# Feed-forward of a streaming encoder layer: running-sum copies and second-layer additions traced with priority, two weight quarters split in pieces of 512 columns

## The chip, the cores and the metric

One NeuronCore of a Trainium2 chip runs the whole program in one launch. The metric is the device time of one execution in microseconds, the median of the runs shown: 977.34 us before the change (three runs, 976.65 to 977.91).

## What is computed

The reference is one layer of a hybrid encoder on two request groups (512 prompt tokens and 64 sample tokens, 576 together, model width 1024): a mixing stage (gated delta rule and differential attention), a cross-attention to a memory, and a feed-forward stage, then a last norm. The change lies in the feed-forward stage:

```
hn = _rmsnorm(h, p['ln_ffn'])
h = h + jnp.square(jax.nn.relu(hn @ p['w_ff1'])) @ p['w_ff2']
```

`w_ff1` is 1024 x 4096 and `w_ff2` is 4096 x 1024, all in float32. The kernel keeps float32 accuracy by splitting each operand into a high part (a cast to a rounded format, `F32R`) and a low part (the operand minus that cast), and adding three products: high x high, high x low, low x high.

## The kernel before, in words

**First layer.** The 4096 hidden columns are taken in 16 pairs of 128-column blocks (`ff1_pair(p, sx)`, L1469). A pair is a 2 x 2 block product: two halves of the model width and two halves of the tokens (`N0`, `N1`, 288 tokens each, `NH`). It is computed with seven block products instead of eight, in a Strassen-like scheme, from sums and differences of the activations (`B1`, `B2`, `T12`, `T34`, prepared earlier by `combine`) and of the weights. One `product(i, b, start)` is 12 matmuls of 288 columns (4 steps over 128 rows of the half width, times three high/low combinations). The order that is traced is 1, 5, 6, 2, 7, 3, 4. Products 1, 6, 7 and 4 go one after another into the same PSUM bank `x` (tag `ba`), which goes on accumulating: after products 1, 6 and 7 the bank holds a running sum that is needed on its own, so `keep(b)` (L1492) copies it to SBUF on ScalarE (L1494) before the next product may add to the bank. Product 5 goes into bank `z` (tag `g1`), is copied by `keep` as well, and product 3 is added later; product 2 has bank `y` (tag `gs`). `put` (L1497) then forms one block of the hidden layer: an addition on VectorE (L1502), relu and square on ScalarE (L1503, L1504), from pair 10 on a multiplication by the squared norm factor (L1506), a cast (L1508) and the low part (L1509).

**Weights of the first layer.** `load_pair(p)` (L1384) starts two loads of 512 KB, `raw` a and b; together they are the four quarters of the block. `split_pair(p)` (L1394) makes the seven weight operands: sums and differences on VectorE (L1402, L1407, L1408, L1415, in place in the raw tiles), and for each operand a cast on ScalarE and a low part on VectorE (`halves_to`, L1355; in the profile the cast is L1356 and the low part L1357). Five of the operands are 512 columns of a partition wide and are split one by one; the quarters in a (operands 6 and 7, tile tag `wl`) and those in b (operands 2 and 4, tag `w4`, shown as `w` in the profile) are split in one instruction of 1024 columns each. The destination tiles are the buffers of the pair that is being multiplied, so a cast can start when the products that read the old contents are done. `ff1_pair(p)` traces `split_pair(p + 1)` and `load_pair(p + 2)` at its end. For pair 0 there is a separate `split_first`, which the change leaves alone.

**Second layer.** The main loop (L1648) has 8 groups of two pairs. In group g, after every `ff1_pair`, four blocks `project(weights2(...), ..., add_group(g - 1, m), kt=4)` (L1653) multiply the hidden block of the group before by 128 columns of `w_ff2`: a first half of 256 tokens, whose bank holds two column halves side by side (the second is the `more` that the evacuation gets), and a second half of 320 tokens. Each half takes a bank of tag `pr`, of which there are three in turn. `weights2` (L1461) loads 256 KB and `split` (L1453) casts it (L1457) and takes the low part (L1458). `add_group` (L1535) gives the evacuation: for group 0 the sum is copied (`A.copy` at L1542, or `add_to` at L191, which copies `more` on ScalarE at L192 and adds on VectorE at L193); for the others it is added on VectorE into the running sum `am` (L1544) and, for the first half, the second part is added as well (L1546). A bank is free when its last reader is done.

**What sets the order.** Each engine runs its own queue in order. The order inside a queue is fixed when the program is built: a scheduler goes through the traced instructions with an estimate of their times and, whenever an engine is free, gives it the ready instruction with the smallest priority number. That number counts up in the order of tracing. Inside `with tc.high_priority():` the count starts again from the beginning of the program, so such an instruction goes ahead of every ready one without it; among themselves they go by their place in their own block. Before the change the casts and low parts in `split_pair` (for p above 1) and in `split` (where `urgent`) are traced so; `keep`, `put` and the evacuations in `add_group` are not.

Of the kernel before, what the change touches and what calls it, by code (L numbers as in the profile page):

```python
# [11 lines left out]
ALU = mybir.AluOpType  # L12
# [25 lines left out]
def hybrid_layer_kernel(  # L38
# [10 lines left out]
    V, A, G = nc.vector, nc.scalar, nc.gpsimd  # L49
# [50 lines left out]
    def bank(tag="ba"):  # L100
        return ps.tile([P, 512], F32, tag=tag, name=nm(tag), bufs=BANKS[tag])
# [4 lines left out]
    def mm(out, lhsT, rhs, start=True, stop=True, pin=False, skip_group_check=False):  # L106
        i = nc.tensor.matmul(out, lhsT, rhs, start=start, stop=stop, skip_group_check=skip_group_check)  # L107
        if pin:
            tc.keep_in_program_order(i)
# [81 lines left out]
    def add_to(dst, b, more):  # L191
        A.copy(dst, more)  # L192
        V.tensor_tensor(dst, b, dst, ALU.add)  # L193
# [302 lines left out]
    for a0, n in HALVES:  # L496
        b = bank("pr")
# [7 lines left out]
    b = bank()  # L505
# [49 lines left out]
    for j in range(3):  # L555
        b = bank()
# [713 lines left out]
    for k2 in range(KT // 2):  # L1270
        b = bank()
# [6 lines left out]
    for h in range(H):  # L1278
# [15 lines left out]
        for t, (q0, _) in enumerate(QT):  # L1294
            t0, n = TT[t]
            kk, kl = (mkT, mkl) if t < 4 else (cmT, cml)
            b = bank(("gs", "g0", "g1")[t % 3])
# [25 lines left out]
        for i in range(2):  # L1323
            b, b2 = bank(("g0", "gs")[i]), bank(("g1", "ba")[i])
# [14 lines left out]
    NH = T // 2  # L1339
# [8 lines left out]
    def ft(tag, shape, bufs, dt=F32):  # L1348
        return fp.tile(shape, dt, tag=tag, name=nm(tag), bufs=bufs)
# [5 lines left out]
    def halves_to(hi, lo, src):  # L1355
        A.copy(hi, src)  # L1356
        V.tensor_tensor(lo, src, hi.bitcast(F32), ALU.subtract)  # L1357
# [21 lines left out]
    def wtile(tag, shape, dt=F32R):  # L1379
        return wp.tile(shape, dt, tag=tag, name=nm(tag), bufs=3 if tag == "raw" else 2)  # L1380
# [3 lines left out]
    def load_pair(p):  # L1384

        raws[p] = raw = [wtile("raw", raw_, F32) for i in range(2)]
        for i in range(2):
            src = w_ff1[0, 512 * i : 512 * i + 512, 2 * P * p : 2 * P * (p + 1)]
            nc.sync.dma_start(raw[i], src.rearrange("(k p) n -> p k n", p=P))

    def low_and_high(t):
        return [t[:, 0], t[:, 1]]

    def split_pair(p):  # L1394


        a, b = raws.pop(p)
        A11, A21, A12 = a[:, :, :P], a[:, :, P:], b[:, :, :P]
        s1 = ft("s1", block_, 2)
        parts[p] = ws = {}  # L1400
        with tc.high_priority() if p > 1 else ExitStack():
            V.tensor_tensor(s1, A21, b[:, :, P:], ALU.add)  # L1402
            ws[1] = low_and_high(wtile("wh", wide_))
            halves_to(*ws[1], A11)
            ws[5] = low_and_high(wtile("wh", wide_))
            halves_to(*ws[5], s1)
            V.tensor_tensor(A21, A11, A21, ALU.subtract)  # L1407
            V.tensor_tensor(A11, s1, A11, ALU.subtract)  # L1408
            t = [wtile("wl", raw_) for _ in range(2)]
            halves_to(*t, a)  # L1410
            ws[6], ws[7] = ([x[:, :, c : c + P] for x in t] for c in (0, P))
            t = [ft("w4", raw_, 3, F32R) for _ in range(2)]
            halves_to(*t, b)
            ws[2], ws[4] = ([x[:, :, c : c + P] for x in t] for c in (0, P))
            V.tensor_tensor(A12, A12, A11, ALU.subtract)  # L1415
            ws[3] = low_and_high(ft("w4", wide_, 3, F32R))
            halves_to(*ws[3], A12)
# [51 lines left out]
    def ff1_pair(p, sx):  # L1469
        ws = parts.pop(p)  # L1470

        def of(x, n):
            return lambda j, k: x[j][:, n, k, :]

        def half(u, n):
            return lambda j, k: u[:, j, k, n]

        operands = {
            1: lambda j, k: B1[k // 2][:, j, k % 2, :], 2: half(B2, N0), 3: half(B2, N1),
            4: of(T34, 1), 5: of(T12, 0), 6: of(T12, 1), 7: of(T34, 0),  # L1480
        }

        def product(i, b, start):
            w, x = ws[i], operands[i]
            for k in range(4):
                for j, (jw, jx) in enumerate(((0, 0), (0, 1), (1, 0))):
                    mm(
                        b[:, :NH], w[jw][:, k, :], x(jx, k),
                        start=start and k == j == 0, stop=k == 3 and j == 2, skip_group_check=True,
                    )  # L1490

        def keep(b):  # L1492
            x = ft("keep", [P, NH], 4)
            A.copy(x, b[:, :NH])  # L1494
            return x

        def put(i, n, b, more):  # L1497
            c = ft("c", [P, NH], 3)
            if more is None:
                A.activation(c, b, AF.Relu)  # L1500
            else:
                V.tensor_tensor(c, b, more, ALU.add)  # L1502
                A.activation(c, c, AF.Relu)  # L1503
            A.activation(c, c, AF.Square)  # L1504
            if p >= 2 * SCALED:
                V.tensor_tensor(c, c, rB[:, n], ALU.mult)  # L1506
            hi, lo = (sx[:, j, 2 * (p % 2) + i, n] for j in range(2))
            A.copy(hi, c)  # L1508
            V.tensor_tensor(lo, c, hi.bitcast(F32), ALU.subtract)  # L1509

        x, y, z = bank("ba"), bank("gs"), bank("g1")
        product(1, x, True)
        s1 = keep(x)
        product(5, z, True)
        s5 = keep(z)
        product(6, x, False)
        s2 = keep(x)
        product(2, y, True)
        put(0, N0, y[:, :NH], s1)
        product(7, x, False)  # L1520
        s3 = keep(x)
        product(3, z, False)
        put(0, N1, z[:, :NH], s2)
        put(1, N1, s3, s5)
        product(4, x, False)
        put(1, N0, x[:, :NH], None)
        put_last[p] = nc.cur_bb.bb.instructions[-1]
        if p + 1 < 2 * NG:
            split_pair(p + 1)
        if p + 2 < 2 * NG:  # L1530
            load_pair(p + 2)
# [3 lines left out]
    def add_group(g, m):  # L1535
        def evac(b, a0, n, more):
            am = (accu[0] if g < SCALED else hT)[m // 4][:, m % 4, a0 : a0 + n]
            if g == 0:
                if more is not None:
                    add_to(am, b, more)  # L1540
                else:
                    A.copy(am, b)  # L1542
                return
            V.tensor_tensor(am, am, b, ALU.add)  # L1544
            if more is not None:
                V.tensor_tensor(am, am, more, ALU.add)  # L1546

        return evac

# [118 lines left out]
    for m in range(KT):  # L1668
# [3 lines left out]
        if m in (3, 4):  # L1672
            t = m - 3
# [43 lines left out]
```

## Time and profile before

| | |
|---|---|
| median of three runs | 977.34 us (976.65 to 977.91) |
| span of the profiled execution, first to last instruction | 975.3 us |
| feed-forward pairs and second-layer blocks | about 571 to 936 us of the span |
| mean granted TensorE clock | 0.998 |
| instructions | 16991, of them 6399 matmuls |

The profiled execution is one of the kernel's runs; its span leaves out what lies before the first and after the last instruction, so 975.3 us stands beside the 977.34 us of the median. PE is TensorE's matmul row and PEld its weight loads, which run beside the matmuls; DVE is VectorE, ACT ScalarE, POOL GpSimd, SPq the queue that issues DMAs. A row of a list of instructions is: start, duration, engine, line, operation, output and inputs, shape; in square brackets how long the engine stood idle before it and on what it had waited ("issue" is time for which the profile shows no release).

### The profile page before, as it was taken

To read this page: it belongs to the slowest core of one execution; us is meant where nothing else is said; L and a number is where in the kernel's file an instruction comes from. 1 tells how busy PE (TensorE), PEld (TensorE's weight loads), DVE (VectorE), ACT (ScalarE), POOL (GpSimd) and SP (SyncE) were. 2 spreads that over 40 slices of the span, in tenths; PEclk is the share of its full clock that TensorE was granted. 3 is DMA by queue.
4 is the path that set the end of the run, shared out by engine and by line. 5 is a ranking of instruction groups with operands and counts; after the bars stand their busy time and mean duration, and the time that the engine had idled before them with its cause. 6 is when DMAs were issued, how large, how long until landed. Compare 5 with 4: busy or idle time off the path is not lost.

```text
span 975.3 us, 16991 instructions
## 1 busy us (share of the span) xinstructions
PE 960.4 (98%) x6399; PEld 889.9 (91%) x6399; DVE 689.4 (71%) x1508; ACT 536.9 (55%) x1218; POOL 66.6 (7%) x158
## 2 busy tenths in 40 slices
PE   9999999998999999999999999999999999999996
PEld 7999998997888878999999999999999999999996
DVE  6655777776867776666657888567867779978674
ACT  6664774533656765435445567665544444545444
POOL 4341020211010000000000000000000000000000
PEclk9999999999999999999999999999999999999999
DMA  7442332120744666341121423332323223322202
GB/s 209 117 138 77 95 125 66 46 64 23 187 122 122 219 182 196 87 130 44 45 65 44 141 69 96 90 88 88 87 81 87 87 87 87 87 87 87 66 23 97
DMA packets 124915, 96.01 MB, mean 98 GB/s; under 512 B 6204, under 2 KB 112846, under 8 KB 124322
## 3 DMA queue, kind: packets, MB, share of 16 engines
q1 hardware_dynamic: 124466, 94.28, 33.6%
q8 instruction: 50, 0.82, 0.4%
q10 hardware_dynamic: 368, 0.66, 0.2%
q14 instruction: 31, 0.25, 0.1%
HBM read 79.93 MB, written 9.75 MB: 92 GB/s over the span
## 4 chain that ended last, share of the span: by engine, by line
PE 58%; issue 2%; DVE 1%; ACT 1%; DMA 0%; POOLq 0%; POOL 0%; ACTq 0%; DVEq 0%; SPq 0%
PE pr L107 37%; PE ba L107 10%; PE g L107 6%; PE gs L107 4%; PE ba L113 1%; DMA raw<-in_w_ff_dram 0%; ACT u L1596 0%; ACT c L1504 0%; DVE u L1552 0%; DVE w2l L1458 0%; ACT c L1503 0%; DVE w L1357 0%; DVE wl L1357 0%; DVE wh L1357 0%; ACT wl L1356 0%
## 5 line engine op out<-in xcount | busy, mean ns | idle before, releaser
L107 PE MATMUL pr<-u,wh 128*128 128x320 f32 (+2 forms) x1240 | 325.9, 341 | 0.1
L107 PE MATMUL pr<-u,wl 128*128 128x256 f32 (+1 forms) x816 | 226.1, 301 | 0.0
L107 PEld LDWEIGHTS pr<-u,wh 128*128 128x128 f32 x1240 | 212.1, 189 | 15.2 <-ACT u L286 0.3
L107 PEld LDWEIGHTS pr<-u,wl 128*128 128x128 f32 x816 | 150.5, 189 | 2.5 <-DVE wl L387 0.2
L160 DVE TENSOR_TENSOR wl<-raw,wh 128x1024 fp32r<-128x1024 f32 x65 | 79.5, 1223 | 56.5 <-ACT wh L159 56.3
L159 ACT CAST wh<-raw 128x1024 fp32r<-128x1024 f32 x65 | 68.2, 1049 | 61.9 <-PE pr L107 46.6
L107 PE MATMUL pr<-u,w2h 128*128 128x320 f32 (+1 forms) x384 | 98.5, 341 | 0.0
L1457 ACT CAST w2h<-r 128x512 fp32r<-128x512 f32 x56 | 34.7, 620 | 87.6 <-PE pr L107 85.4
L107 PE MATMUL pr<-f,w2h 128*128 128x320 f32 (+1 forms) x288 | 74.5, 341 | 0.5 <-DVE u L1546 0.5
L107 PEld LDWEIGHTS pr<-u,w2h 128*128 128x128 f32 x384 | 65.0, 188 | 4.5 <-ACT u L1542 0.3
L107 PE MATMUL pr<-u,w2l 128*128 128x256 f32 (+1 forms) x256 | 65.2, 296 | 0.0
L1544 DVE TENSOR_TENSOR u<-u,pr 128x256 f32<-128x256 f32 x96 | 42.4, 450 | 17.1 <-PE pr L107 16.5
L206 POOL TENSOR_TENSOR tiny<-tiny,nhalf 128x1 f32<-128x1 f32 (+4 forms) x10 | 8.8, 879 | 651.3 <-DVE tiny L1610 514.1
L107 PE MATMUL ba<-u,wl 128*128 128x288 f32 x360 | 52.9, 296 | 0.0
L107 PEld LDWEIGHTS pr<-f,w2h 128*128 128x128 f32 x288 | 48.8, 188 | 4.5 <-issue 1.7
L107 PEld LDWEIGHTS ba<-u,wl 128*128 128x128 f32 x360 | 49.2, 188 | 0.6 <-ACT keep L1494 0.5
L107 PE MATMUL pr<-f,w2l 128*128 128x256 f32 (+1 forms) x192 | 48.9, 295 | 0.0
L107 PEld LDWEIGHTS pr<-u,w2l 128*128 128x128 f32 x256 | 47.0, 189 | 1.5
L1458 DVE TENSOR_TENSOR w2l<-r,w2h 128x512 fp32r<-128x512 f32 x56 | 38.5, 688 | 9.6 <-ACT w2h L1457 9.4
L107 PE MATMUL pr<-wh,u 128*128 128x512 f32 x128 | 41.6, 400 | 0.1
L1503 ACT ACTIVATE c<-c 128x288 f32<-128x288 f32 x48 | 20.6, 443 | 28.5 <-DVE c L1502 28.5
L107 PEld LDWEIGHTS pr<-f,w2l 128*128 128x128 f32 x192 | 35.2, 189 | 1.1
(552 smaller groups left out, 2024.8 us busy)
## 6 DMA issues: line engine op xcount, KB each, us to landing
raw<-in_w_ff_dram SPq DMA_DIRECT2D x36, 512.0 KB
raw<-in_w_in_dram SPq DMA_DIRECT2D x28, 512.0 KB
r<-in_w_ff_dram SPq DMA_DIRECT2D x56, 256.0 KB
raw<-in_w_mem_k_dram SPq DMA_DIRECT2D x8, 512.0 KB
raw<-in_w_mem_v_dram SPq DMA_DIRECT2D x8, 512.0 KB
raw<-in_w_out_dram SPq DMA_DIRECT2D x8, 512.0 KB
raw<-in_w_mem_q_dram SPq DMA_DIRECT2D x8, 512.0 KB
raw<-in_w_mem_o_dram SPq DMA_DIRECT2D x8, 512.0 KB
```

Of the source, the lines that this page charges most:

```text
L107: i = nc.tensor.matmul(out, lhsT, rhs, start=start, stop=stop, skip_group_check=skip_group_check)
L113: i = nc.tensor.transpose(out, in_, ident[:n, :n])
L159: A.copy(wh, raw)
L160: V.tensor_tensor(wl, raw, wh.bitcast(F32), ALU.subtract)
L206: G.tensor_tensor(out, in_, bc(nhalf[: in_.shape[0], 0:1], list(in_.shape)), ALU.pow)
L1457: A.copy(wh, src)
L1458: V.tensor_tensor(wl, src, wh.bitcast(F32), ALU.subtract)
L1503: A.activation(c, c, AF.Relu)
L1544: V.tensor_tensor(am, am, b, ALU.add)
```

## The change

Three edits, all in the feed-forward stage.

1. `split_pair`: the cast and the low part of a and of b are made in two pieces of 512 columns each (two of the four row blocks at a time) instead of one instruction of 1024 columns. 
2. `keep`: the copy of the running sum is traced under `tc.high_priority()`.
3. `add_group`: the copies and additions of the evacuation are traced under `tc.high_priority()`, in both branches.

```
             t = [wtile("wl", raw_) for _ in range(2)]
-            halves_to(*t, a)
+            for i in range(2):
+                halves_to(*(x[:, 2 * i : 2 * i + 2] for x in t), a[:, 2 * i : 2 * i + 2])
             ws[6], ws[7] = ([x[:, :, c : c + P] for x in t] for c in (0, P))
             t = [ft("w4", raw_, 3, F32R) for _ in range(2)]
-            halves_to(*t, b)
+            for i in range(2):
+                halves_to(*(x[:, 2 * i : 2 * i + 2] for x in t), b[:, 2 * i : 2 * i + 2])
             ws[2], ws[4] = ([x[:, :, c : c + P] for x in t] for c in (0, P))
...
         def keep(b):
             x = ft("keep", [P, NH], 4)
-            A.copy(x, b[:, :NH])
+            with tc.high_priority():
+                A.copy(x, b[:, :NH])
             return x
...
             if g == 0:
+                with tc.high_priority():
+                    if more is not None:
+                        add_to(am, b, more)
+                    else:
+                        A.copy(am, b)
+                return
+            with tc.high_priority():
+                V.tensor_tensor(am, am, b, ALU.add)
                 if more is not None:
-                    add_to(am, b, more)
-                else:
-                    A.copy(am, b)
-                return
-            V.tensor_tensor(am, am, b, ALU.add)
-            if more is not None:
-                V.tensor_tensor(am, am, more, ALU.add)
+                    V.tensor_tensor(am, am, more, ALU.add)
```

## The prediction

> **What bounds the kernel now.** I read the page's first and fourth parts, then the busy time by stage, then who TensorE's weight loads waited for in the feed-forward, and last the lists of instructions around those waits.
>
> ```profile
> span 975.3 us, 16991 instructions
> PE 960.4 (98%) x6399; PEld 889.9 (91%) x6399; DVE 689.4 (71%) x1508; ACT 536.9 (55%) x1218; POOL 66.6 (7%) x158
> ...
> PE 58%; issue 2%; DVE 1%; ACT 1%; DMA 0%; POOLq 0%; POOL 0%; ACTq 0%; DVEq 0%; SPq 0%
> ```
>
> ```profile
> core 0: us, PE busy (x) PEld busy (x) DVE busy (x) ACT busy (x) POOL busy (x), PEclk, DMA share, GB/s
> 571.00:936.00 365.00, 364.18 (x2490) 349.02 (x2489) 273.92 (x518) 197.06 (x422) 0.00 (x0) 1.00 0.29 85
> 813.00:837.00 24.00, 24.00 (x166) 23.13 (x166) 23.06 (x46) 11.96 (x25) 0.00 (x0) 1.00 0.31 88
> ```
>
> TensorE bounds it: matmuls are in flight in 364.18 of the 365.00 us of the feed-forward at full clock, while VectorE is busy 75% and ScalarE 54% of them. So the change can only win what TensorE loses in waits there, and can only lose by making TensorE wait. A wait of TensorE shows as idle time of the weight loads:
>
> ```profile
> PEld ba L107 <- ACT keep L1494: 2.5, 10, 0.3
> PEld pr L107 <- issue: 1.9, 7, 0.7
> PEld pr L107 <- ACT u L1542: 0.3, 1, 0.3
> PEld ba L107 <- DVE u L1357: 0.2, 1, 0.2
> ```
>
> Those are all its waits from 571 to 936 us: 4.9 us (2.5 + 1.9 + 0.3 + 0.2). Ten are for the copy of a running sum, 0.25 us each; eight are for a bank `pr` of the second layer (the 1.9 has no release shown; the rows of the second edit below say why I read it so). No wait is for a weight operand of the first or second layer except the last 0.2 us, which is an activation's low part and is not touched.
>
> The Trainium skill, in "Perfetto Trace Analysis" (Identifying the Most-Contended Engine), says that matmul busy time misjudges how near the roofline a kernel is and that the busy share of the weight loads should be used. By that the loads' idle time here, 365.00 - 349.02 = 16.0 us, would be the room, and the sum below would be three times larger. The trace does not agree that it can be won by this change: only 4.9 us of it has a wait that ends on another engine's work.
>
> **Edit 2, the copies with priority.** One of the ten waits, in two views of the same moment:
>
> ```profile
> 697.87 1.74 PE L107 MATMUL ba<-u,wl 128*128 128x288 f32 x12
> 699.45 1.76 PE L107 MATMUL g<-u,w 128*128 128x288 f32 x12
> ...
> 699.51 0.43 ACT L1508 CAST f<-c 128x288 fp32r<-128x288 f32 x1
> 699.85 1.04 ACT L1356 CAST wl<-raw 128x1024 fp32r<-128x1024 f32 x1
> 700.80 0.39 ACT L1494 COPY keep<-ba 128x288 f32<-128x288 f32 x1
> ...
> 701.24 0.83 PEld L107 LDWEIGHTS ba<-u,w 128*128 128x128 f32 x6 [0.27 <-ACT keep L1494]
> ```
>
> Product 7 ends at 699.61 (697.87 + 1.74). At that moment two things become ready on ScalarE: the copy of the running sum, and the cast of quarter a for the next pair, whose tile product 7 has just finished reading. The cast has priority and the copy has not, so the copy starts 1.2 us late, at 700.80, and product 4, which may not add to the bank before, starts 0.27 us late. Between the two products that share the bank lies one other product, 1.59 us (699.45 - 697.87 is 1.58). With the change the copy has the first place of its block and the cast a later one, so the copy starts when ScalarE is free at 699.85 and ends near 700.25, 0.8 us before it is needed. The other copies behind a cast lose less now (a 512-column cast of 0.62 us) and gain the same order. The whole 2.5 us goes; what is late next is product 3 itself, so nothing.
>
> What the copy passes is casts and low parts of the next pair's weights, later by up to 0.39 us for each of four copies. Their cover: the cast of quarter a at 699.85 feeds products 6 and 7 of the next pair, about 19 us later (a period of 24.34 us, below, after this pair's product 6). If the cover were gone, it would cost 0.39 us a time. No DMA is issued by the copies; the loads of `raw`, which wait for the split to end, would be issued up to 1.5 us later, and who waits for them is the sum L1402 on VectorE, not TensorE.
>
> **Edit 3, the additions with priority.** A wait for a bank:
>
> ```profile
> 656.64 0.41 DVE L1544 TENSOR_TENSOR u<-u,pr 128x256 f32<-128x256 f32 x1
> 657.14 0.69 DVE L1357 TENSOR_TENSOR w<-raw,w 128x512 fp32r<-128x512 f32 x1
> 657.75 0.82 DVE L1509 TENSOR_TENSOR u<-c,u 128x288 fp32r<-128x288 f32 x2
> 658.48 0.69 DVE L1458 TENSOR_TENSOR w2l<-r,w2h 128x512 fp32r<-128x512 f32 x1
> 659.08 0.41 DVE L1546 TENSOR_TENSOR u<-u,pr 128x256 f32<-128x256 f32 x1
> ```
>
> ```profile
> 659.61 0.30 PEld L107 LDWEIGHTS pr<-f,w2h 128*128 128x128 f32 x2 [0.19 <-issue]
> ...
> 861.71 0.30 PEld L107 LDWEIGHTS pr<-f,w2h 128*128 128x128 f32 x2 [0.72 <-issue]
> ```
>
> The first addition of a bank is done at 657.05, the second starts only at 659.08, after four low parts, and TensorE's loads go on at 659.61, right after it ends (659.49). That is why I count "issue" as waits for this bank. With priority the second addition follows the first: ended by about 657.5, 2 us early. The longest, 0.72 us, has the same shape (low parts ahead of an L1546). All of it, 1.9 + 0.3 = 2.2 us, is for work that now goes first. The bank is needed two halves later (one block, 3.17 us of matmuls by the row quoted further down), and the longest that an addition can still wait is one running operation, some 0.7 us, and its sister's 0.41.
>
> What it passes: low parts of the second-layer weights (L1458), of the hidden blocks (L1509), and the split's sums. Each is put back by at most two additions, 0.83 us. They have this cover:
>
> ```profile
> ACT w2h L1457 <- PE pr L107: 85.4, 38, 4.4
> ```
>
> The second-layer casts wait 85.4 us for TensorE to give back a buffer, so they run as soon as a buffer is free, one block or more ahead of their use, and not because ScalarE is late. Without that cover the price would be 0.83 us for each of 56 blocks.
>
> **Edit 1, the pieces.**
>
> ```profile
> L1356 ACT CAST w<-raw 128x1024 fp32r<-128x1024 f32 x15 | 15.8, 1052 | 0.8
> L1356 ACT CAST w<-raw 128x512 fp32r<-128x512 f32 x15 | 9.2, 613 | 0.8 <-DVE raw L1415 0.2
> ...
> L1357 DVE TENSOR_TENSOR w<-raw,w 128x1024 fp32r<-128x1024 f32 x15 | 18.4, 1225 | 2.5 <-ACT c L1503 2.4
> L1357 DVE TENSOR_TENSOR w<-raw,w 128x512 fp32r<-128x512 f32 x15 | 10.3, 689 | 1.8 <-ACT w L1356 1.3
> ```
>
> Two quarters in each of 15 pairs: 30 casts become 60, each pair of pieces 2 x 613 - 1052 = 0.17 us longer, 5.2 us in all on ScalarE; 30 low parts become 60, 2 x 689 - 1225 = 0.15 us longer, 4.6 us in all on VectorE. That is 202 of 365 us on ScalarE and 279 on VectorE: hidden beside TensorE. It adds no wait of a new kind; a low part of a first piece can start 0.44 us sooner. Its use is a bound: if the program's order still puts a cast ahead of a copy, the copy is held 0.61 us at most and ends 0.61 + 0.39 = 1.0 us after its product, inside the 1.59 us. So the 2.5 us has two covers.
>
> **The sum.** From the waits: 2.5 + 2.2 = 4.7 us. A second way is the time from one pair's end to the next pair's end, seen in the chain of waits by the start of the block that follows product 4, and from what a period would take without waits:
>
> ```profile
> 639.81 3.17 PE pr L107 x20
> ...
> 650.92 1.60 PE g L107 x12
> ...
> 654.42 4.58 PE pr L107 x28
> ...
> 678.76 4.56 PE pr L107 x28
> ...
> 875.57 4.36 PE pr L107 x27
> ...
> 899.61 4.34 PE pr L107 x27
> ```
>
> ```profile
> 628.23 0.43 PEld L107 LDWEIGHTS ba<-u,w 128*128 128x128 f32 x3 [0.26 <-ACT keep L1494]
> ...
> 776.45 0.43 PEld L107 LDWEIGHTS ba<-u,w 128*128 128x128 f32 x3 [0.27 <-ACT keep L1494]
> ```
>
> A period is seven products and four blocks, 7 x 1.59 + 4 x 3.17 = 23.81 us with no wait. Early periods take 678.76 - 654.42 = 24.34 us, a late one, which has no copy or bank wait in the list, 899.61 - 875.57 = 24.04. Seven of the ten copy waits are in such early periods, one in each, of 0.26 to 0.27 us (the first and the last of the seven stand above). If these seven periods come only down to the late one, that is 7 x 0.30 = 2.1 us; the remaining three copy waits add 2.5 - 7 x 0.27 = 0.6 and the long bank wait 0.7 to 0.9: 3.5 us. So the gain is 3.5 to 4.7 us and I take 4.2, a little above the middle, since both kinds of wait lose their cause altogether. Against the profiled execution that is 975.3 - 4.2 = 971.1 us of span; the median stands 2.0 us above the span, so 977.34 - 4.2 = 973.1 us. If all fourteen periods came to 23.81 us, 14 x 0.23 = 3.2 us more than the 3.5 could be won: 970.6 us.
>
> **Rivals.** (a) The waits move. The order in every queue, TensorE's too, is worked out anew from estimated times; in this profile it already had five matmuls of the next pair's first product drawn forward, just before the wait at 659.61. If new waits of 0.25 us stand in 14 periods, 3.5 us come back: 976.6 us, no change that can be told. For it: every queue is ordered by estimates that this trace shows to be off by tenths of a us. Against it: both kinds of wait become shorter by more than 0.5 us.
>
> (b) Slower: VectorE becomes the bound in the periods with the merge of the running sums (L1552, L1553). In 813 to 837 us it is busy 23.06 of 24.00. The pieces add 0.31 us a pair, so 23.37 of a period of 23.8 to 24.0; the point from which it decides is 0.4 us of VectorE waiting for casts within such a period. Then low parts come late and TensorE waits as at 861.71, 0.72 us, and with the additions in front the backlog falls on weights: at one wait of 0.72 us in each of 14 periods 10.1 - 4.2 = 5.9 us slower, 983.2 us. Against it: only five periods are as full, and the margin of the weights is microseconds.
>
> In "VectorE: DVE Perf Modes" (The TRN2 errata) the Trainium skill says that small tiles pay a fixed latency each and that pieces should be large. The rows of edit 1 agree (0.17 and 0.15 us); by that rule the pieces cost up to 9.8 us of engine time, 987 us if nothing hid it, which is rival (b) in its extreme.
>
> (c) The change does nothing: copies and casts come out in the old order, because in the estimate the cast is ready a moment sooner. Then the pieces alone still cut the 1.04 us hold to 0.61. Only if the additions too stay where they were does the time remain 977.3 us.
>
> **How the numbers follow.** About 0.2% (2.0 us) is what a measurement of this kernel can tell from no change. Forecast 0.72 (973.1, own range 970.6 to 975.3). (a) with (c) 0.20 (975.4 to 979.3, likeliest 976.6). (b) 0.08. So faster 0.72, same 0.20, slower 0.08. The range for 8 in 10 goes from 971.3, a little inside the extreme of 970.6, up to 977.6, into (a) and (c).
>
> **What would show it.** Right: in the waits of the weight loads from 571 to 936 us no line for `keep`, and less than 0.5 us of "issue"; a copy L1494 right after its product with the cast behind it; L1546 right after L1544; no cast or low part of 128x1024 left at L1356 and L1357; the early periods near 23.9 us. Wrong: the listed waits gone but periods still above 24.2 us (a); VectorE above 23.5 of 24 us with TensorE waiting for `w2l` or `wl` (b); casts still ahead of copies (c).

## The result, and the profile after

The changed kernel takes 972.39 us (median of four runs, 971.19 to 973.01) beside 977.25 us for the kernel before on the same chip: a ratio of 0.9949, 95% interval 0.9935 to 0.9963, so 3.6 to 6.4 us less. A second measurement, together with other kernels, gave 970.99 us and 0.994 (0.9927 to 0.9952). The change is faster, by more than the 0.2% that can be told.

The head of the page of the changed kernel:

```profile
span 968.8 us, 17030 instructions
PE 954.5 (99%) x6399; PEld 888.5 (92%) x6399; DVE 689.6 (71%) x1538; ACT 541.3 (56%) x1248; POOL 66.9 (7%) x158
```

There are 30 instructions more on VectorE and 30 more on ScalarE, as counted, and the span is 6.5 us shorter (968.8 against 975.3). This profiled execution is the shortest of the four: their spans are 968.8 to 970.0 us. The whole list of what TensorE's weight loads waited for, from 571 to 936 us:

```profile
PEld pr L107 <- issue: 0.2, 1, 0.2
```

The ten waits for a copy are gone, and of the eight for a bank one is left. An early copy, the one that follows product 7 of its pair as in the prediction's example (ScalarE, then TensorE):

```profile
696.70 0.43 ACT L1511 CAST f<-c 128x288 fp32r<-128x288 f32 x1
697.04 0.40 ACT L1497 COPY keep<-ba 128x288 f32<-128x288 f32 x1
697.33 1.15 ACT L1356 CAST wl<-raw 128x512 fp32r<-128x512 f32 x2
```

```profile
695.05 1.74 PE L107 MATMUL ba<-u,wl 128*128 128x288 f32 x12
696.63 1.76 PE L107 MATMUL g<-u,w 128*128 128x288 f32 x12
698.23 1.76 PE L107 MATMUL ba<-u,w 128*128 128x288 f32 x12
```

Product 7 ends at 696.79 (695.05 + 1.74), the copy starts at 697.04 and ends at 697.44, the two pieces of the cast follow, and product 4 starts at 698.23, straight behind product 3. The additions on VectorE:

```profile
654.24 0.41 DVE L1549 TENSOR_TENSOR u<-u,pr 128x256 f32<-128x256 f32 x1
654.57 0.45 DVE L1512 TENSOR_TENSOR u<-c,u 128x288 fp32r<-128x288 f32 x1
654.94 0.41 DVE L1551 TENSOR_TENSOR u<-u,pr 128x256 f32<-128x256 f32 x1
```

One low part stands between this bank's two additions where there were four. The prediction's sign, L1546 (now L1551) right after L1544 (now L1549), is met only nearly: the second addition reads the sum that the first writes, and in most blocks one other instruction lies between them. The chain of waits shows what this makes of the periods:

```profile
652.33 12.69 PE pr L107 x80
...
676.16 12.69 PE pr L107 x80
...
869.17 12.69 PE pr L107 x80
...
893.00 12.69 PE pr L107 x80
```

The four second-layer blocks of a period are now one unbroken run of TensorE of 12.69 us (4 x 3.17), and a period takes 23.83 us early (676.16 - 652.33) and late (893.00 - 869.17). It was 24.34 and 24.04.

### The profile page after: what moved, and what is told of

It reads as the page before. It is cut to its first block, busy times and chain, and to the rows that moved or that the text cites. A ratio compares the mean times of both kernels' runs of the same rounds, so it can differ in the third digit from the quotient of the medians.

```text
span 968.8 us, 17030 instructions
## 1 busy us (share of the span) xinstructions
PE 954.5 (99%) x6399; PEld 888.5 (92%) x6399; DVE 689.6 (71%) x1538; ACT 541.3 (56%) x1248; POOL 66.9 (7%) x158
## 4 chain that ended last, share of the span: by engine, by line
PE 61%; issue 2%; ACT 0%; POOLq 0%; POOL 0%; DVE 0%; ACTq 0%
PE pr L107 38%; PE ba L107 11%; PE g L107 7%; PE gs L107 4%; PE ba L113 1%; ACT u L1601 0%; POOLq L1718 0%; POOL tiny L206 0%; DVE u L1219 0%; ACTq L1606 0%; DVE tiny L1615 0%; POOLq L206 0%
## 5 line engine op out<-in xcount | busy, mean ns | idle before, releaser
L107 PEld LDWEIGHTS pr<-u,wh 128*128 128x128 f32 x1240 | 211.8, 188 | 15.4 <-ACT u L286 0.4
L107 PE MATMUL pr<-f,w2h 128*128 128x320 f32 (+1 forms) x288 | 72.4, 339 | 0.0
L1549 DVE TENSOR_TENSOR u<-u,pr 128x256 f32<-128x256 f32 x96 | 43.3, 451 | 8.6 <-PE pr L107 7.9
```

## The experiments

Three theories stood against each other. Theory A: TensorE waits because copies and additions stand behind casts and low parts in fixed queues, and their rank in the queue is the cause. Theory B or P: the size of the pieces matters, for good or ill. Theory C: the gain is the new order of TensorE's own queue. The kernel before was run again on each chip (977.58, 977.11 and 977.08 us); ratios are to that, with 95% intervals.

**The pieces alone.** Edit: only the first edit of the change.

> The two quarters in pieces of 512 columns, nothing else. Theory A (order decides: the copy of a running sum waits because casts with priority go first; each wait of TensorE costs its listed idle time and some 0.1 us of restart): in the built order both pieces of quarter a still stand ahead of the copy, so the copy is held 1.2 us instead of 1.04; the seven waits of 0.27 us grow to about 0.45 us and the bank waits stay: 978 to 979 us, 1 to 1.7 us above 977.3. The prediction's second cover (a copy is held by one piece of 0.61 us at most) would mean no copy wait is left: 973.5 to 974.5 us. Theory B (the gain of the changed kernel beyond the 4.7 us of listed waits comes from shorter pieces): 975.5 to 976 us.

Measured: 976.14 us, 0.9986 (0.9977 to 0.9994). Waits of the weight loads:

```profile
PEld ba L107 <- ACT keep L1496: 3.7, 15, 0.5
PEld pr L107 <- issue: 1.0, 5, 0.2
```

ScalarE, and the loads of TensorE, at one such wait:

```profile
699.43 1.14 ACT L1356 CAST wl<-raw 128x512 fp32r<-128x512 f32 x2
700.48 0.39 ACT L1496 COPY keep<-ba 128x288 f32<-128x288 f32 x1
```

```profile
700.50 0.19 PEld L107 LDWEIGHTS pr<-u,w2h 128*128 128x128 f32 x1
700.92 1.63 PEld L107 LDWEIGHTS ba<-u,w 128*128 128x128 f32 x12 [0.23 <-ACT keep L1496]
```

Both pieces go ahead of the copy, back to back (x2, 1.14 us), so the copy is held at least as long as before and the copy waits grow from 2.5 to 3.7 us. That is theory A's reading of the order, and the "second cover" is refuted. The bank waits shrink from 2.2 to 1.2 us (beside the 1.0 shown there is one of 0.2), so the sum of the list stays at 4.9 us. Yet the time fell by 1.4 us where A expected a rise: one matmul of the second layer (the load at 700.50) had been drawn ahead of product 4 and filled part of the wait. The two pinned runs below test whether that is the reason. The Trainium skill says in "Perfetto Trace Analysis" (Optimizing Scalar/DVE Operations) that breaking up instructions may let work complete sooner where an engine that is not full causes bubbles elsewhere; here the trace agrees only in part, since the pieces did nothing for the copy while both outranked it.

**The copies alone.** Edit: only the second edit of the change.

> Only the copy of the running sum with priority; quarters in one instruction of 1024 columns, additions without priority. Theory A: the line for keep goes from TensorE's waits, 10 waits of 0.25 us and 0.1 us of restart each, 3.5 us: 973.5 to 974.3 us; the bank waits stay at about 2 us. Theory B (pieces are needed for it): a 1024-column cast that is already running when the product ends still holds the copy, half of the waits stay: 975.5 us. Theory C (the re-ranked order of TensorE, not the waits, made the gain): less than 1 us, 976.5 us.

Measured: 973.1 us, 0.9955 (0.9942 to 0.9967).

```profile
PEld pr L107 <- DVE u L1545: 1.8, 2, 1.3
PEld ba L107 <- ACT keep L1495: 0.7, 1, 0.7
```

One copy wait is left of ten, in the second pair. So a 1024-column cast need not be cut: theory B fails, and so does theory C, which gave this edit less than 1 us. Theory A's range began 0.4 us too high. Three bank waits remain: the two shown and one of 0.2 us for L1543.

**The additions alone.** Edit: only the third edit.

> Only the second-layer copies and additions with priority. Theory A: bank waits (1.9 us issue and 0.3 us for L1542) go, eight waits with 0.1 us of restart each, 3.0 us: 974.0 to 974.8 us; the copy waits stay at 2.5 us. Theory C: with the banks free early no matmul of the next pair is drawn forward and the order of TensorE is the traced one, so most of the 5 us comes with this edit alone: 972.5 to 973.5 us.

Measured: 974.51 us, 0.9968 (0.9957 to 0.998).

```profile
PEld ba L107 <- ACT keep L1494: 2.3, 9, 0.3
PEld ba L107 <- DVE u L1357: 0.2, 1, 0.2
```

The lines for banks, "issue" among them, are gone and the copy waits stand: the idle time without a shown release had been for banks. The periods, by the chain of waits, are 24.10 us early:

```profile
654.02 12.66 PE pr L107 x80
...
678.12 12.69 PE pr L107 x80
```

That is 0.27 us above 23.83, the copy wait as listed (0.27). So a copy wait costs what the list gives it; the 0.1 us of restart that theory A added to each wait does not show. The time lies in theory A's range, and theory C's, 972.5 to 973.5 us, is missed by 1.0 us.

**Both priorities, no pieces; the changed kernel; four pieces.** The first was run twice. Edit of the last: `for i in range(4)` and `x[:, i : i + 1]` in place of `range(2)` and `x[:, 2 * i : 2 * i + 2]`.

> Both priorities, quarters in one instruction of 1024 columns. Theory A: as the changed kernel, 972.0 to 972.8 us; the pieces are worth nothing, periods of 23.83 us. Theory B: the pieces carry a part, 973.5 to 974.5 us, with waits for copies or banks behind 1.04 and 1.22 us instructions left in the list.

> The changed kernel once more, to stand on the same chip and in the same rounds as the three below: 972.4 us, 0.995 of the kernel before.

> Both priorities without the pieces, again. Theory A (pieces are worth nothing once the copies go first): equal to the changed kernel within 0.7 us, and the 0.9 us that lie between 971.5 and 972.4 so far are scatter. Theory P (many small pieces pay a fixed latency each, and a part of it reaches TensorE): 0.8 to 1.0 us below the changed kernel again.

> The changed kernel with the two quarters in four pieces of 256 columns: per pair some 0.8 us more of ScalarE and 0.6 us more of VectorE than in the changed kernel. Theory A: hidden, within 0.7 us of the changed kernel, periods of 23.83 us. Theory P: twice as many pieces again cost twice as much, 1 to 2 us above it.

Measured: both priorities without pieces 971.49 us, 0.9939 (0.9925 to 0.9953), and again 972.65 us, 0.9947 (0.9933 to 0.996); the changed kernel beside the latter 970.99 us, 0.994 (0.9927 to 0.9952); four pieces 971.42 us, 0.9942 (0.9929 to 0.9954). Without pieces was the faster in one comparison and the slower in the other, and four pieces is level with two. The list of waits of the first run without pieces has one line, the activation's low part that no edit touches:

```profile
PEld ba L107 <- DVE u L1357: 0.2, 1, 0.2
```

In its second run there are two bank waits more, 0.2 and 0.5 us, at 855 and 857 us; the last section says what lies behind them. The kernel with four pieces has one copy wait of 0.5 us. The pieces neither help nor cost anything that these runs can tell (some 1 us). The casts that four pieces make take 404 ns for 256 columns against 621 for 512, so the fixed part is real, and hidden.

**TensorE held to the traced order**, with the kernel before and with the pieces alone. Edit, in all matmuls of `product` and of the blocks in the main loop (`project` hands `pin` on to its matmuls; that part is left out here):

```
                     mm(
                         b[:, :NH], w[jw][:, k, :], x(jx, k),
-                        start=start and k == j == 0, stop=k == 3 and j == 2, skip_group_check=True,
+                        start=start and k == j == 0, stop=k == 3 and j == 2, skip_group_check=True, pin=True,
...
-            project(weights2(...), (pend,), add_group(g - 1, m), kt=4)
+            project(weights2(...), (pend,), add_group(g - 1, m), kt=4, pin=True)
```

> The kernel before, with the matmuls of the pairs and of the second-layer blocks held to the order in which they are traced (no priorities added, no pieces), so that TensorE draws no matmul of the next pair or block forward. Theory A (the gain is the waits, and the order of TensorE only hides a part of some): no gain; waits for copies in all periods, the late ones too, about 14 of 0.27 us, and bank waits somewhat longer: 977 to 979.5 us. Theory C (the new order of TensorE makes the gain): 973 to 975 us.

> The pieces alone, with TensorE held to the traced order. The pieces alone took 1.4 us off, though TensorE waited longer for copies (3.7 us in the list instead of 2.5); its order had one second-layer matmul drawn ahead of product 4. Theory A: that matmul hid 0.24 us of each copy wait; without it the waits are 0.45 us in 14 periods and the gain turns into a loss: 978.5 to 981 us. Rival: the pieces help VectorE finish the additions sooner, and the gain stays: 975.5 to 976.5 us.

Measured: 995.63 us, 1.0188 (1.0172 to 1.0203), and 989.71 us, 1.0131 (1.0117 to 1.0145). Both are far slower, and both lie beyond every expectation, theory A's too. The list of the first, from 565 to 965 us:

```profile
PEld pr L107 <- DVE u L1544: 8.8, 5, 1.8
PEld pr L107 <- PE pr L107: 5.6, 6, 1.0
PEld ba L107 <- ACT keep L1494: 4.5, 14, 0.9
PEld ba L107 <- issue: 3.3, 1, 3.3
PEld pr L107 <- ACT u L1542: 1.0, 2, 0.7
PEld ba L107 <- DVE u L1357: 0.2, 1, 0.2
```

The line of 3.3 us is one place, the block of norm factors, where TensorE, held in order, waits for VectorE from 710.07 to 713.32 us (loads); the list of the matmuls' own waits names the releaser:

```profile
PE ba L107 <- DVE tiny L1643: 3.2, 1, 3.2
```

What follows it in the same kernel, in windows (the third number from the end is the granted clock):

```profile
712.00:714.00 2.00, 0.65 (x3) 0.68 (x4) 1.20 (x4) 0.00 (x0) 0.00 (x0) 0.64 0.88 276
714.00:716.00 2.00, 2.00 (x10) 1.95 (x10) 0.14 (x1) 0.57 (x1) 0.00 (x0) 0.50 0.19 57
716.00:720.00 4.00, 4.00 (x17) 3.66 (x16) 0.93 (x3) 0.02 (x1) 0.00 (x0) 0.58 0.00 0
```

From 714 to 720 us the clock costs another 2.7 us (2 x 0.50 + 4 x 0.42), so this place takes 6.0. Without it the first kernel would stand at 989.6 us, level with the second, which has neither this wait nor the dip. The second's list, over the same stretch:

```profile
PEld pr L107 <- DVE u L1546: 9.6, 6, 1.8
PEld ba L107 <- ACT keep L1496: 6.2, 15, 0.8
PEld pr L107 <- PE pr L107: 3.9, 5, 0.8
```

So the fixed order costs 12.6 us in both (989.71 - 977.08), and the lists agree roughly: 20.1 and 19.7 us against 4.9. The pieces make the copies wait longer here too (6.2 against 4.5 us), as theory A says, and the banks less (13.5 against 8.8 + 5.6 + 1.0 = 15.4), and the two cancel. The rise of the total that theory A expected came in neither order. The same queue of VectorE as in the prediction's wait for a bank, in the pinned kernel, and TensorE's wait for it (in the loads, then in the matmuls, where L1546 is named):

```profile
767.51 0.69 DVE L1458 TENSOR_TENSOR w2l<-r,w2h 128x512 fp32r<-128x512 f32 x1
768.11 0.41 DVE L1546 TENSOR_TENSOR u<-u,pr 128x256 f32<-128x256 f32 x1
```

```profile
768.64 0.30 PEld L107 LDWEIGHTS pr<-f,w2h 128*128 128x128 f32 x2 [0.95 <-PE pr L107]
768.67 0.53 PE L107 MATMUL pr<-f,w2h 128*128 128x320 f32 x2 [0.67 <-DVE u L1546]
```

VectorE does the same four low parts before its L1546, but TensorE waits 0.95 us instead of 0.19: the five matmuls of the next pair that the kernel before draws forward there (0.65 us) are what hid most of the rest. So the 4.9 us of listed waits in the kernel before were what was left after the scheduler's reordering of TensorE had hidden the larger part. The 1.4 us of the pieces alone are gone with the order fixed, which fits a reordering as their source; no run shows it by itself. Nor was the changed kernel run with TensorE held to the traced order, so what its gain would be there is open.

**The casts lowered instead of the copies raised.** The edit takes the priority from everything in `split_pair`, the sums included:

```
-        with tc.high_priority() if p > 1 else ExitStack():
+        with ExitStack():
```

> The kernel before, with the priority taken from the casts and low parts of the first-layer weights instead of given to the copies and additions. If the rank of cast against copy is all that matters, the copies now come first by their place in the trace and their waits go: 973.5 to 974.5 us. But in the built order the 1024-column cast of quarter a still stands ahead of the third copy in every pair, since it is ready when ScalarE is free; by theory A the waits of 0.27 us therefore stay: 976.5 to 977.5 us.

Measured: 972.43 us, 0.9953 (0.9939 to 0.9967). My expectation by theory A was wrong. The ScalarE queue in an early period:

```profile
697.91 0.43 ACT L1508 CAST f<-c 128x288 fp32r<-128x288 f32 x1
698.25 0.39 ACT L1494 COPY keep<-ba 128x288 f32<-128x288 f32 x1
698.54 1.05 ACT L1356 CAST wl<-raw 128x1024 fp32r<-128x1024 f32 x1
```

The copy goes first by its place in the trace, with no priority at all; the expectation rested on the late pairs, where the cast still stands ahead. Periods there are 23.96 us (823.05 - 799.09 in the chain of waits), early ones 23.84. The bank waits fell too (0.2 us is left in the list), though the additions were not raised: the split's low parts no longer outrank them. So rank is the cause, and it can be set from either side. Why the cast stays ahead in the late pairs was not tried.

**More work for VectorE.** Two kernels, both the changed one with 32 extra reductions over 576 columns (748 ns each) from group 4 on; the result is not used. First without priority on a table that is ready early (`rB`), then after each block on the sum just added, with priority (the second edit is shown; `pad` is a tile of one column):

```
+            if g > 3:
+                am = (accu[0] if g - 1 < SCALED else hT)[m // 4][:, m % 4, :]
+                with tc.high_priority():
+                    V.tensor_reduce(pad, am, AX.X, ALU.max)
```

> The changed kernel with 32 extra reductions over 576 columns on VectorE, one for each second-layer block from group 4 on, whose result is not used: some 0.7 us each, 2.8 us in each period of 23.83 us from about 726 us on. VectorE is busy 22.7 of 23.8 us in the two fullest periods of the changed kernel, so it would be asked for 25.5 there. Theory A (the weights and the additions have microseconds of margin, so a VectorE that is full for two periods catches up in the next): at most 1 us more, 972 to 973.5 us. The prediction's rival (b), VectorE as the bound with a wait of 0.72 us each time: at least the excess of 1.7 us in two periods and waits in the others, 975.5 to 977 us.

> The changed kernel with 32 extra reductions over 576 columns on VectorE, one after each second-layer block from group 4 on, reading the sum that was just added and traced with priority, so that they cannot be put into idle time elsewhere: 0.75 us each, 3.0 us a period from about 726 us on. In the two fullest periods (797 to 845 us) VectorE is then asked for 25.7 and 25.2 us of 23.83. Theory A (margins of microseconds, a backlog is made up in the next period): at most 1.5 us above the changed kernel, 971 to 973 us. Rival (b) of the prediction: the excess of 1.9 + 1.3 us is on the path and banks or weights come late as at 861.71 before: 974.5 us or more.

Measured: 971.18 us, 0.9941 (0.9928 to 0.9953), and 972.82 us, 0.9955 (0.9943 to 0.9968). The first decides little, since the scheduler put 31 of the 32 reductions between 712 and 772 us, where VectorE had room. One of these periods:

```profile
725.76:749.60 23.84, 23.84 (x167) 23.11 (x166) 23.08 (x45) 12.06 (x28) 0.00 (x0) 1.00 0.30 89
```

(fourth number: VectorE, busy 23.08 of 23.84 us with no wait of TensorE). In the second VectorE is busy 21.8 to 23.2 us in each of four periods of 23.8 running (797.5 to 892.8 us). TensorE waits three times for an addition, 2.1 us in all, 1.73 of it in one place; VectorE's queue and TensorE's loads there:

```profile
850.95 0.68 DVE L1357 TENSOR_TENSOR w<-raw,w 128x512 fp32r<-128x512 f32 x1
853.33 0.69 DVE L1402 TENSOR_TENSOR s<-raw,raw 128x512 f32<-128x512 f32 x1 [1.70 <-DMA raw<-in_w_ff_dram]
853.94 0.48 DVE L1550 TENSOR_TENSOR u<-u,pr 128x320 f32<-128x320 f32 x1
854.33 0.42 DVE L1552 TENSOR_TENSOR u<-u,pr 128x256 f32<-128x256 f32 x1
```

```profile
854.47 0.30 PEld L107 LDWEIGHTS pr<-f,w2h 128*128 128x128 f32 x2 [1.73 <-DVE u L1550]
```

The wait comes while VectorE stands idle: at the head of its queue is the sum L1402, which waits 1.70 us for a load, and the additions are behind it. Rival (b) has its place here, with 3 us more work a period than the change gives, and its price is one wait of 1.73 us and two of 0.2, not one in each period.

## Why the prediction was right, and where it was not

**What bounds the kernel, and the sum.** Right in place: what was won was lost time of TensorE in the feed-forward. In the chains of waits the last run of blocks before it starts at 525.77 us before the change and at 525.41 after. The long run of second-layer matmuls at its end, before and after:

```profile
923.26 27.57 PE pr L107 x168
```

```profile
916.84 27.51 PE pr L107 x168
```

So 6.1 of the 6.5 us of span lie between. Low in size: the forecast was 4.2 us, and the list of waits holds 4.9. The medians give 4.9 and, in the second measurement, 6.1 us. That 973.1 lies so near 972.39 is in part luck: the forecast put 2.0 us between median and span, and in the changed kernel's four runs 1.8 to 3.7 us lie outside the span (972.5 - 968.8 in the profiled one), which made up for part of the larger gain.

**Where the size was off.** The sum took 24.04 us of a late period as what early periods come down to, because that period had no listed wait. It had shorter ones, below what the list shows. At 873.70 us the loads of product 4 start 0.14 us after the load before them has ended, just when the copy ends (873.26 + 0.39) that stands behind a 1024-column cast. And the four blocks of that period, cut up by drawn-forward matmuls, take 0.23 + 4.36 + 3.24 + 5.01 = 12.84 us instead of 12.69; how much of this is waiting is not shown. Both went: all periods are at 23.83 or 23.84 us, beside the 23.81 of the prediction's extreme, but for the one with the norm factors (26.06 us; 26.54 before) and one of 23.95. That route should have been the main one, with the listed waits as its lower end.

**The copies.** Right in mechanism, low in size: 2.5 us was expected, and the copies alone took 4.5 us off (3.2 to 5.7 us by the interval's ends, 0.9967 and 0.9942 of 977.58), 3.4 us by the spans. The list of waits fell by 2.0 us only. The rest shows in the periods: several are at 23.83 us with the four blocks unbroken (12.69 us), though the additions had no priority, and the bank waits fell in number from eight to three (2.2 to 2.0 us). So the two edits overlap: alone they took off 4.5 and 3.1 us, both together 6.1 and 4.5 us in two measurements. With intervals of over 1 us to each side, the runs do not say by how much.

**The additions.** Right: 2.2 us was expected, the additions alone took 3.1 us off, and "issue" was the bank: its line went with this edit, and for the longest of these waits the list of the matmuls' own waits, of the kernel before, names the addition:

```profile
PE pr L107 <- DVE u L1546: 0.5, 1, 0.5
```

One reading was incomplete. The longest wait, 0.72 us at 861.71, was put down to low parts ahead of an L1546. In the kernel before, VectorE had stood idle 0.90 us for a load some 3 us ahead of that place, as the next row shows, and was busy from there on without a break. The one wait left after the change is in the same period (23.95 us), where VectorE stands 1.78 us for the same load:

```profile
857.50 0.69 DVE L1402 TENSOR_TENSOR s<-raw,raw 128x512 f32<-128x512 f32 x1 [0.90 <-DMA raw<-in_w_ff_dram]
```

```profile
852.93 0.69 DVE L1402 TENSOR_TENSOR s<-raw,raw 128x512 f32<-128x512 f32 x1 [1.78 <-DMA raw<-in_w_ff_dram]
```

**The pieces.** Right that they are hidden (two and four pieces level with none). Wrong that they are a second cover for the copies: a copy is not held by one piece but by both, since both outrank it.

**The rivals.** (a) The waits did not move; 0.2 us is left. But TensorE's drawn-forward matmuls, mentioned there as a sign of poor estimates, were in truth the cover that kept some 13 us of waits out of the kernel before. (b) did not happen with the change's load; its "five periods as full" was a misreading, since in the windows of the kernel before only two come near (23.06 us of 24.00, and 21.91 of 25.00 from 837 to 862 us). (c) did not happen.

## What to carry to other kernels

In a kernel whose bound engine is 98% busy, work out a period from that engine's own unbroken stretches, and take the difference to the measured period as the most that can be won; the listed waits are less, since short ones are not in the list. A scheduler that reorders the bound engine hides part of every late release, so the list also changes with the order: 4.9 us here, 20 us with the order held. Give the instructions that release an accumulator a rank above work that is needed a period later (or give that work none): raising the one and lowering the other came to the same within some 1 us (971.0 to 972.7, and 972.4 us). Cutting the long instruction into pieces does nothing for a waiting reader while all pieces outrank it.

## What the runs showed that was not expected

Holding TensorE to the traced order cost 12.6 us (989.71 against 977.08), about twice what the change gained or more, and in one of two kernels 6.0 more at a single place: 3.2 us without a matmul, and a granted clock of 0.50 to 0.58 in the windows from 714 to 720 us. The Trainium skill says in "TensorE: Matmul & The Clock Gate" (Part 1: The HAM clock gate) that the array falls to half its clock after an idle window of about 3.4 us and comes back after as long a busy one. The trace agrees in kind. In narrow windows the clock falls within 712.5 to 712.75 us, 2.4 us after the last of ten matmuls of one column each (708.98 to 710.15), so the stretch without a matmul before the fall was shorter than the page's; whether these small matmuls count as idle is not shown. It is back to full between 719.2 and 719.4 us, 6 us after the first matmul at 713.35, later than by the page's figure.

An instruction at the head of VectorE's queue that waits for a load holds ready additions behind it: in the same late period VectorE stood idle for it 0.90 us before the change, 1.78 after, 1.70 with the extra reductions. The size of it is not the change's doing: in a second execution of the changed kernel it stood 0.42 us and TensorE had no wait there, and in two executions of the kernel without pieces 0.58 and 2.19 us, the latter with the two bank waits at 855 and 857 us.
